# A row softmax on one core: the first tile's load cut into pieces of one, three and twelve rows a partition in place of four and twelve

## The chip, the cores and the metric

The kernel runs on one core of a Trainium2 chip. The metric is the device time of one execution in microseconds (us). Executions of the same kernel agree within about 0.8% here (the kernel with two tiles in one-row pieces varies more); each comparison below was run beside the kernel before on the same chip.

## The reference

```python
x: (16, 1024, 512) float32
x_scaled = x / 0.5
exp_x = np.exp(x_scaled - np.max(x_scaled, axis=-1, keepdims=True))
out = exp_x / np.sum(exp_x, axis=-1, keepdims=True)      # float32
```

There are 16,384 rows of 512 numbers. 33.55 MB come in and 33.55 MB go out, and nothing can be left out: every input byte is read once and every output byte written once.

## The kernel before

The rows are cut into 8 tiles of 128 partitions x 16 rows (4.19 MB each), with six buffers. A tile is worked on in blocks of rows: VectorE takes each row's maximum, ScalarE the exponentials with their sums, VectorE and ScalarE divide the rows of the block before and the one before that, and a tile is stored when its last block is done. The sync queue (SP) issues all loads, ScalarE's queue all stores.

```python
    FIRST = [(0, 4), (4, 16)]                  # pieces in which tile 0 is loaded
    BLOCKS_FIRST = [(0, 4), (4, 4), (8, 8)]    # (first row, rows): blocks of tile 0
    BLOCKS = [(0, 8), (8, 8)]                  # blocks of the other tiles
    data = ctx.enter_context(tc.tile_pool(name="data", bufs=6))
    # ... cut ...
    def load(c):
        xt = tiles[c] = data.tile([P, G, D], fp32, name="xt")
        for lo, hi in FIRST if c == 0 else [(0, G)]:
            nc.sync.dma_start(out=xt[:, lo:hi, :], in_=xr[c][:, lo:hi, :])

    def shift(i):                              # one block
        c, b, B = blocks[i]
        xb = tiles[c][:, b : b + B, :]
        negmax = stats.tile([P, 8], fp32, name="negmax")
        nc.vector.tensor_reduce(negmax[:, 0:B], xb, axis=AX, op=MAX, negate=True)
        # ... cut ...
    def store(i):
        c, b, B = blocks[i]
        if b + B == G:
            nc.scalar.dma_start(out=outr[c], in_=tiles[c])

    for i in range(n + 3):
        if i < n:
            if blocks[i][1] == 0:
                load(blocks[i][0])
            shift(i)
            exponentials(i)
        if 1 <= i <= n:
            scale_vector(i - 1)
        if 2 <= i <= n + 1:
            scale_scalar(i - 2)
        if 3 <= i:
            store(i - 3)
```

Of the kernel before, what the change touches and what calls it, by code (L numbers as in the profile page):

```python
# [1 line left out]

# [4 lines left out]


@with_exitstack
def kernel(  # L10
    ctx: ExitStack,
    tc: tile.TileContext,
    x: bass.AP,
    out: bass.AP,
):
    nc = tc.nc
    fp32 = mybir.dt.float32
    P = nc.NUM_PARTITIONS
    AX = mybir.AxisListType.X
    EXP = mybir.ActivationFunctionType.Exp  # L20
    COPY = mybir.ActivationFunctionType.Copy
    MAX = mybir.AluOpType.max

    D = x.shape[-1]
    xf = x.flatten_outer_dims()
    of = out.flatten_outer_dims()
    N = xf.shape[0]




    G = 16
    C = N // (P * G)
    assert C * P * G == N
    xr = xf.rearrange("(c p g) d -> c p g d", p=P, g=G)
    outr = of.rearrange("(c p g) d -> c p g d", p=P, g=G)

    FIRST = [(0, 4), (4, 16)]
    BLOCKS_FIRST = [(0, 4), (4, 4), (8, 8)]
    BLOCKS = [(0, 8), (8, 8)]  # L40

    data = ctx.enter_context(tc.tile_pool(name="data", bufs=6))
    stats = ctx.enter_context(tc.tile_pool(name="stats", bufs=6))

    ctx.enter_context(tc.manual_schedule())


    warm = stats.tile([P, 1], fp32, name="warm", bufs=1)
    nc.vector.memset(warm, 0.0)  # L49
    nc.scalar.activation(out=warm, in_=warm, func=EXP)  # L50

    tiles = {}
    blocks = [(c, b, B) for c in range(C) for b, B in (BLOCKS if c else BLOCKS_FIRST)]
    state = {}
# [6 lines that stand above are left out]
    def shift(i):  # L61
# [4 lines that stand above are left out]
        bias = stats.tile([P, 8], fp32, name="bias")  # L66
        nc.vector.tensor_scalar_mul(bias[:, 0:B], negmax[:, 0:B], 2.0)  # L67
        state[i] = (xb, bias)

    def exponentials(i):  # L70
        B = blocks[i][2]
        xb, bias = state[i]
        sums = stats.tile([P, 8], fp32, name="sums")
        for g in range(B):
            nc.scalar.activation(  # L75
                out=xb[:, g, :],
                in_=xb[:, g, :],
                func=EXP,
                bias=bias[:, g : g + 1],
                scale=2.0,  # L80
                accum_out=sums[:, g : g + 1],
            )
        state[i] = (xb, sums)

    def scale_vector(i):
        B = blocks[i][2]
        xb, sums = state[i]
        recip = stats.tile([P, 8], fp32, name="recip")
        nc.vector.reciprocal(recip[:, 0:B], sums[:, 0:B])  # L89
        for g in range(B - B // 4):  # L90
            nc.vector.tensor_scalar_mul(xb[:, g, :], xb[:, g, :], recip[:, g : g + 1])  # L91
        state[i] = (xb, recip)

    def scale_scalar(i):
        B = blocks[i][2]
        xb, recip = state[i]
        for g in range(B - B // 4, B):
            nc.scalar.activation(  # L98
                out=xb[:, g, :], in_=xb[:, g, :], func=COPY, scale=recip[:, g : g + 1]
# [7 lines that stand above are left out]
    n = len(blocks)  # L107
# [14 lines that stand above are left out]
# [1 line left out]
_INS = ['x']  # L123
_OUTS = [((16, 1024, 512), 'float32')]


# [23 lines left out]
```

## Time and profile before

The kernel before took 162.37 us, the median of three runs (162.35 to 162.6). The span that the profile covers is about 2 us shorter.

| | value | read from |
|---|---|---|
| span | 160.4 us | page |
| DMA, 2 to 158 us | share 1.00, 430 GB/s | table of windows |
| VectorE (DVE) busy | 114.0 us, 71% | page |
| ScalarE (ACT) busy | 113.1 us, 70% | page |
| first reduction starts | 5.43 us | timeline |
| first store issued | 43.59 us | timeline |

These lines are from the page of the kernel before. The digits are busy tenths in 40 slices of 4.0 us. The lines of q1 (loads) and q10 (stores) give packets, MB, and the time that the packets took as a share of 16 DMA engines' span. The last two lines are the chain of work that ended last, by engine and by line (L65 is the reduction).

```profile
span 160.4 us, 517 instructions
...
DVE  0608999999999999999999949996199946000000
ACT  3072579989999999999999995799709999100000
...
DMA  5999999999999999999999999999999999999993
GB/s 190 464 425 490 392 417 490 403 392 507 409 368 417 386 441 474 392 417 474 417 409 476 417 400 490 417 400 458 441 409 441 458 409 433 458 400 425 474 409 155
DMA packets 2451, 67.13 MB, mean 419 GB/s; under 512 B 272, under 2 KB 272, under 8 KB 272
...
q1 hardware_dynamic: 1296, 33.56, 49.4%
q10 hardware_dynamic: 1152, 33.55, 48.5%
...
DMA 43%; DVE 34%; ACT 7%; issue 1%; SPq 0%
DMA xt<-in_x_dram 24%; DVE negmax L65 23%; DMA out_dram<-xt 19%; DVE xt L91 9%; ACT xt L75 5%; ACT xt L98 2%; DVE bias L67 1%; DVE recip L89 0%; SPq L59 0%
```

DMA reads 9 in 38 of 40 slices, while VectorE and ScalarE have zeros near both ends. (A packet, here one partition's share of a load or store, is counted whole in the slice where it starts, so the GB/s of single slices scatter around the mean.) The two queues sum to 97.9% of 160.4 us: the DMA engines were busy for 157.0 us and idle for 3.4, nearly all of it before the first packet and after the last. The chain names VectorE's reductions with 23% of the span. DMA has more of the chain than any other engine, 43%. A chain shows one path of waits; it doesn't say that the resource it crosses is the one in short supply.

The table of windows has, for one stretch, its length, busy time of VectorE, ScalarE and GpSimd, the clock, the DMA share and GB/s:

```profile
2.00:158.00 156.00, 113.94 (x147) 111.78 (x290) 0.00 (x0) 1.00 1.00 430
```

From the timeline (start us, us, engine, line, operation, idle time before and what ended it):

```profile
0.73 3.43 SPq L59 DMA_DIRECT2D xt<-in_x_dram  x7
...
5.43 2.29 DVE L65 TENSOR_REDUCE negmax<-xt 128x4 f32<-128x2048 f32 x1 [4.57 <-DMA xt<-in_x_dram]
...
43.59 0.37 ACTq L105 DMA_DIRECT2D out_dram<-xt  x1
```

The first seven loads, thus tiles 0 to 5, are issued by 4.16 us, long before the first result. The first store follows at 43.59 us, the last at 137.05 us; no computation comes after it, but packets move until 159.2 us. Until the first store only loads move, and they have some 58 us of transfers to make (25.2 MB at 430 GB/s, an estimate). The list of DMA issues gives count, KB each, and us from issue to landing:

```profile
xt<-in_x_dram SPq DMA_DIRECT2D x1, 3072.0 KB, 11.5
xt<-in_x_dram SPq DMA_DIRECT2D x1, 1024.0 KB, 4.7
```

### The profile page before, as it was taken

How to read it: one execution, taken by the hardware profiler on the slowest of the kernel's cores; microseconds unless marked ns; L12 is line 12 of the kernel's file. 1: busy time of each engine (PE TensorE's matmuls, PEld its weight loads, DVE VectorE, ACT ScalarE, POOL GpSimd, SP SyncE). 2: the span in 40 equal slices, each digit the busy share in tenths (PEclk: the TensorE clock that was granted, in tenths of full speed). 3: DMA queues.
4: the chain of work that ended last, by engine and by line, in shares of the span. 5: the costliest groups of instructions: out<-in, count | busy, mean ns of one | idle time of the engine just before them, and what ended most of it. 6: DMA issues, size and time to landing. Idle time of an engine off the chain costs nothing.

```text
span 160.4 us, 517 instructions
## 1 busy us (share of the span) xinstructions
DVE 114.0 (71%) x148; ACT 113.1 (70%) x290; POOL 0.2 (0%) x4
## 2 busy tenths in 40 slices
DVE  0608999999999999999999949996199946000000
ACT  3072579989999999999999995799709999100000
POOL 0000000000000000000000000000000000000000
DMA  5999999999999999999999999999999999999993
GB/s 190 464 425 490 392 417 490 403 392 507 409 368 417 386 441 474 392 417 474 417 409 476 417 400 490 417 400 458 441 409 441 458 409 433 458 400 425 474 409 155
DMA packets 2451, 67.13 MB, mean 419 GB/s; under 512 B 272, under 2 KB 272, under 8 KB 272
## 3 DMA queue, kind: packets, MB, share of 16 engines
q1 hardware_dynamic: 1296, 33.56, 49.4%
q10 hardware_dynamic: 1152, 33.55, 48.5%
q14 instruction: 3, 0.02, 0.0%
HBM read 33.55 MB, written 33.55 MB: 418 GB/s over the span
## 4 chain that ended last, share of the span: by engine, by line
DMA 43%; DVE 34%; ACT 7%; issue 1%; SPq 0%
DMA xt<-in_x_dram 24%; DVE negmax L65 23%; DMA out_dram<-xt 19%; DVE xt L91 9%; ACT xt L75 5%; ACT xt L98 2%; DVE bias L67 1%; DVE recip L89 0%; SPq L59 0%
## 5 line engine op out<-in xcount | busy, mean ns | idle before, releaser
L75 ACT ACTIVATE xt<-xt,bias 128x512 f32<-128x512 f32 x128 | 90.5, 708 | 23.2 <-DVE bias L67 23.2
L65 DVE TENSOR_REDUCE negmax<-xt 128x8 f32<-128x4096 f32 (+1 forms) x17 | 70.8, 4163 | 16.9 <-DMA xt<-in_x_dram 16.9
L91 DVE TENSOR_SCALAR xt<-xt,recip 128x512 f32<-128x512 f32 x96 | 39.6, 482 | 0.6
L75 ACT ACTIVATION_READ_ACCUMULATOR xt<-xt,bias 128x1 f32 x128 | 23.9, 187 | 0.0
L98 ACT ACTIVATE xt<-xt,recip 128x512 f32<-128x512 f32 x32 | 21.0, 707 | 0.0
L89 DVE RECIPROCAL recip<-sums 128x8 f32<-128x8 f32 (+1 forms) x17 | 3.3, 192 | 3.2 <-ACT xt L75 3.2
L67 DVE TENSOR_SCALAR bias<-negmax 128x8 f32<-128x8 f32 (+1 forms) x17 | 2.9, 171 | 0.6
L50 ACT ACT_TABLE_LOAD x1 | 1.3, 1283 | 0.7 <-PEq L134 0.7
L49 DVE MEMSET warm<- 128x1 f32 x1 | 0.1, 59 | 0.8 <-PEq L134 0.8
L50 ACT ACTIVATE warm<-warm 128x1 f32<-128x1 f32 x1 | 0.2, 203 | 0.0
L134 POOL MEMSET const-bfloat16-1.0<- 128x1 bf16 x1 | 0.1, 102 | 0.0
L134 POOL MEMSET const-uint8-127<- 128x1 uint8 x1 | 0.1, 101 | 0.0
L134 POOL MEMSET const-float32-0.0<- 128x1 f32 x1 | 0.1, 99 | 0.2 <-issue 0.2
L134 POOL MEMSET const-float32-1.0<- 128x1 f32 x1 | 0.1, 98 | 0.0
## 6 DMA issues: line engine op xcount, KB each, us to landing
out_dram<-xt ACTq DMA_DIRECT2D x8, 4096.0 KB, 26.2
xt<-in_x_dram SPq DMA_DIRECT2D x7, 4096.0 KB, 30.3
xt<-in_x_dram SPq DMA_DIRECT2D x1, 3072.0 KB, 11.5
xt<-in_x_dram SPq DMA_DIRECT2D x1, 1024.0 KB, 4.7
```

Of the source, the lines that this page charges most:

```text
L49: nc.vector.memset(warm, 0.0)
L50: nc.scalar.activation(out=warm, in_=warm, func=EXP)
L65: nc.vector.tensor_reduce(negmax[:, 0:B], xb, axis=AX, op=MAX, negate=True)
L67: nc.vector.tensor_scalar_mul(bias[:, 0:B], negmax[:, 0:B], 2.0)
L75: nc.scalar.activation(out=xb[:, g, :], in_=xb[:, g, :], func=EXP, bias=bias[:, g : g + 1], scale=2.0, accum_out=sums[:, g : g + 1],)
L89: nc.vector.reciprocal(recip[:, 0:B], sums[:, 0:B])
L91: nc.vector.tensor_scalar_mul(xb[:, g, :], xb[:, g, :], recip[:, g : g + 1])
L98: nc.scalar.activation(out=xb[:, g, :], in_=xb[:, g, :], func=COPY, scale=recip[:, g : g + 1])
L134: nc = _bacc.Bacc("TRN2", target_bir_lowering=False, num_devices=1)
```

## The change

Its intent is to have the first data land sooner, so that the computation can start sooner. The whole diff:

```diff
-    FIRST = [(0, 4), (4, 16)]
+    FIRST = [(0, 1), (1, 4), (4, 16)]
     BLOCKS_FIRST = [(0, 4), (4, 4), (8, 8)]
```

The blocks stay as they are. The first reduction still covers four rows, and waits for both small pieces.

## The prediction

> **What bounds the kernel now.** The DMA engines. The page's 40 slices show DMA busy 9 (90% or more) in all but the first and the last slice; the table of windows gives a DMA share of 1.00 and 430 GB/s from 2 to 158 us. The program moves 33.55 MB in and 33.55 MB out, and 67.11 MB at 430 GB/s is 156 us of the span of 160.4. The Trainium skill ("Perfetto Trace Analysis", Roofline) gives about 435 GB/s as the most that one core's 16 DMA engines move; the 430 of this trace agrees. VectorE (114.0 us, 71%) and ScalarE (113.1 us, 70%) have slack. The chain of waits passes through 23% VectorE max reductions, but transfers are always queued behind it: six tiles' loads (25 MB, some 58 us) at the start, later stores and loads.
>
> **What the change does.** The compared order of instructions is the same on every compute engine. Only the load queue differs: a load of 128x2048 becomes one of 128x512 and one of 128x1536, so ten loads in place of nine. The block list is unchanged: the first block is still four rows, and the first reduction now waits for two semaphores, those of the one-row piece and of the three-row piece. So no computation can start on the one row early.
>
> **Costs.**
> - DMA time: in the trace an 8 KB packet takes 309 ns and a 24 KB packet 912 ns; the line through them has 7.5 ns fixed per packet (estimate). Each engine handles 8 packets more, 8 x 7.5 ns, and one semaphore write of 9 ns more: about 0.07 us.
> - Issue: one load issue is 0.33 to 0.57 us on the sync queue. The second piece is issued while the first (0.26 MB, about 0.65 us at the busy rate) moves, so I expect no starvation; later loads are issued about 0.4 us later, behind a long backlog.
> - Start-up: the first 1 MB takes about 3.3 us of packets where 8 x 309 ns would be 2.5 us. Smaller packets in this phase may gain or lose a few tenths of a us.
> - Semaphore lanes shift: the sixth tile's load now waits for the one-row piece to land (about 3.5 us). It would have been issued near 4 us anyway, and has some 40 us of transfers ahead of it: nothing.
>
> **On the critical path.** The DMA stream: +0.07 us, with ±0.4 us for start-up. The first reduction starts at 5.43 us before; I expect 5.3 to 5.9 us. VectorE's work up to the first store's issue (43.6 us) may shift by as much, with no effect on the end, because the queue isn't empty.
>
> **Predicted:** 162.45 us, range 161.9 to 163.0. Chance of faster by over 2%: 0.01; within 2%: 0.97; slower by over 2%: 0.02.
>
> **What the profile would show.** 128 packets of 2 KB and 128 of 6 KB in place of 128 of 8 KB; packets up by 144; DMA share 1.00 from 2 to 158 us; the first reduction at 5.3 to 5.9 us after a wait for the load; first store near 43.6 to 44 us; busy times of VectorE and ScalarE unchanged; span 160.2 to 161.
>
> **What would make it wrong.** If the DMA queue runs dry in some stage (then a compute shift of tenths of a us would show at the end, still far under 2%); if small packets at the start stall the engines for longer than the second piece's issue; if the changed semaphore lanes hold back a load or store late in the program; or if another chip runs the same kernel some tenths of a us differently.

## The result, and the profile after

The changed kernel took 162.47 us (median of four runs, 162.33 to 162.5), the kernel before 162.49 us beside it. The ratio is 0.9991, with a 95% interval of 0.9968 to 1.0015: the same. Ratios here are the mean time of one kernel's runs over that of the other's runs of the same rounds, so not quite the ratio of the medians quoted. Executions over 1.5% slower than the fastest of the same kernel are left out of the means.

The same lines of the page, of the changed kernel:

```profile
span 160.7 us, 519 instructions
...
DMA  5999999999999999999999999999999999999993
GB/s 168 467 404 487 424 400 465 434 408 449 441 318 432 443 400 449 457 400 432 457 408 443 449 416 432 457 408 424 465 416 408 465 432 408 449 449 408 449 449 147
DMA packets 2595, 67.13 MB, mean 418 GB/s; under 512 B 288, under 2 KB 288, under 8 KB 544
...
q1 hardware_dynamic: 1440, 33.56, 49.5%
q10 hardware_dynamic: 1152, 33.55, 48.4%
```

There are 144 more packets, all on the load queue: 128 more of data and 16 semaphore writes. The queues sum to 97.9% of 160.7 us, or 157.3 us busy and 3.4 idle, as before. The same window:

```profile
2.00:158.00 156.00, 113.94 (x147) 111.78 (x290) 0.00 (x0) 1.00 1.01 430
```

The timeline and the list of DMA issues of the changed kernel:

```profile
0.73 4.33 SPq L59 DMA_DIRECT2D xt<-in_x_dram  x8
...
6.12 2.29 DVE L65 TENSOR_REDUCE negmax<-xt 128x4 f32<-128x2048 f32 x1 [5.26 <-DMA xt<-in_x_dram]
...
44.24 0.37 ACTq L105 DMA_DIRECT2D out_dram<-xt  x1
```

```profile
xt<-in_x_dram SPq DMA_DIRECT2D x1, 3072.0 KB, 11.7
xt<-in_x_dram SPq DMA_DIRECT2D x1, 768.0 KB, 4.9
xt<-in_x_dram SPq DMA_DIRECT2D x1, 256.0 KB, 2.6
```

The one-row piece landed 2.6 us after its issue, but no computation begins then. The eighth load of the list, tile 5's, is among the eight issued by 5.06 us, so its new wait for the one-row piece did not hold it. One thing is off: the first reduction began at 6.12 us, 0.69 us later than before and later than the 5.3 to 5.9 predicted. The first store came 0.65 us later too. The span grew by only 0.3 us.

### The profile page after: what moved, and what is told of

Its sections match the earlier page's. It is cut to its first block, busy times and chain, and to the rows that moved or that the text cites. A ratio compares the mean times of both kernels' runs of the same rounds, so it can differ in the third digit from the quotient of the medians.

```text
span 160.7 us, 519 instructions
## 1 busy us (share of the span) xinstructions
DVE 114.0 (71%) x148; ACT 113.1 (70%) x290; POOL 0.2 (0%) x4
## 2 busy tenths in 40 slices
DMA packets 2595, 67.13 MB, mean 418 GB/s; under 512 B 288, under 2 KB 288, under 8 KB 544
## 4 chain that ended last, share of the span: by engine, by line
DMA 43%; DVE 34%; ACT 7%; issue 1%; SPq 1%
DMA xt<-in_x_dram 24%; DVE negmax L65 23%; DMA out_dram<-xt 19%; DVE xt L91 9%; ACT xt L75 5%; ACT xt L98 2%; DVE bias L67 1%; SPq L59 1%; DVE recip L89 0%
```

## The experiments

The theory: the 16 DMA engines set the time. They have work queued from the first packet to the last, so moving the computation's start by microseconds, either way, changes nothing, and the change adds only the small cost of more packets. The first rival: the computation's chain sets the time, and the change failed only because no block used the early row. The second rival, about the size: small pieces cost much more, or nothing at all.

### Let a block use the early row

```diff
     FIRST = [(0, 1), (1, 4), (4, 16)]
-    BLOCKS_FIRST = [(0, 4), (4, 4), (8, 8)]
+    BLOCKS_FIRST = [(0, 1), (1, 3), (4, 4), (8, 8)]
```

> The changed kernel, with the first block of four rows cut into one of one row and one of three, so that something uses the one-row piece. Theory (the DMA stream sets the time, and the early row had no user): the first reduction starts near 3.5 us in place of 6.1, and the time stays within 0.3 us of the kernel before, 162.2 to 162.8 us. Rival (the computation's start sets the time, the change only lacked a block to use it): about 2.5 us less, near 160 us.

It took 162.72 us (162.37 to 163.67, six runs) against 162.56, ratio 1.0024 (0.9996 to 1.0053). Its first two reductions and its first store in the timeline:

```profile
3.47 0.69 DVE L65 TENSOR_REDUCE negmax<-xt 128x1 f32<-128x512 f32 x1 [2.61 <-DMA xt<-in_x_dram]
...
5.88 1.75 DVE L65 TENSOR_REDUCE negmax<-xt 128x3 f32<-128x1536 f32 x1 [1.53 <-DMA xt<-in_x_dram]
...
44.09 0.37 ACTq L105 DMA_DIRECT2D out_dram<-xt  x1
```

The computation did start at 3.47 us, 2 us earlier than in the kernel before, and the time did not fall. The rival wanted 160 us. So the missing block explains why nothing started early. But the early start did not travel: the second reduction waited for the three-row piece until 5.88 us, the third for the twelve-row piece until 13.18 us (12.69 before), and the first store came 0.5 us later than in the kernel before. The run shows that an early row alone moves nothing behind the first block; what an earlier first store would be worth, it doesn't test. That the time doesn't hang on the computation's start rests on the delays that follow.

### Start the computation later: first tile in one piece

```diff
-    FIRST = [(0, 4), (4, 16)]
+    FIRST = [(0, 16)]
```

> The kernel before, with the first tile loaded in one piece of sixteen rows, so that the first reduction starts some 7 us later (near 12.5 us). Theory (DMA stream): 162.2 to 162.8 us, first store near 50 us in place of 43.6. Rival (computation's start sets the time): about 169 us.

It took 162.76 us (162.6 to 163.28, four runs), ratio 1.0015 (0.9992 to 1.0038).

```profile
12.98 2.29 DVE L65 TENSOR_REDUCE negmax<-xt 128x4 f32<-128x2048 f32 x1 [12.12 <-DMA xt<-in_x_dram]
...
46.99 0.38 ACTq L105 DMA_DIRECT2D out_dram<-xt  x1
```

The first reduction came 7.55 us later (12.98 against 5.43), the first store only 3.40 us later, not the 6.4 expected: in the kernel before, VectorE waits once more, 4.76 us, for the twelve-row piece, and that wait is gone here. By the end the delay is gone: the last store is issued at 135.74 us, against 137.05, since VectorE waited 2.57 and 4.98 us for the last two tiles before, and 0 and 2.92 us here. The ratio differs from 1 by 0.15%, and its interval holds 1.

### Start it later still, with the same bytes

The first reduction is done four or ten times; the result is the same and so is every load.

```diff
-        nc.vector.tensor_reduce(negmax[:, 0:B], xb, axis=AX, op=MAX, negate=True)
+        for _ in range(4 if i == 0 else 1):       # 10 in the other kernel
+            nc.vector.tensor_reduce(negmax[:, 0:B], xb, axis=AX, op=MAX, negate=True)
```

> The kernel before, with the first reduction done four times, all computation 6.9 us later at its start, no byte changed. In the kernel before, VectorE waits 2.6 and 5.0 us for the last two tiles, and the stores issued at 122.7 us still find some 2 MB queued (bytes issued less bytes moved at 430 GB/s, an estimate), so a delay of about 5 us at the end has room. Theory (DMA stream): the delay is absorbed, 162.2 to 163.2 us. Rival (computation's start sets the time): 169.3 us.

With four it took 162.50 us (162.43 to 162.7, four runs), ratio 0.9997 (0.9973 to 1.0022). Timeline, then page:

```profile
5.39 9.25 DVE L66 TENSOR_REDUCE negmax<-xt 128x4 f32<-128x2048 f32 x4 [4.53 <-DMA xt<-in_x_dram]
...
46.34 0.38 ACTq L106 DMA_DIRECT2D out_dram<-xt  x1
```

```profile
DMA  5999999999999999999999999999999999999994
```

6.9 us of added VectorE work delayed the first store by only 2.75 us, because the 4.76 us wait for the twelve-row piece is gone here too. It cost nothing measurable.

> The kernel before, with the first reduction done ten times (same result), 9 x 2.29 = 20.6 us later for all computation, and no byte changed. Theory (DMA stream, fed by six queued tiles): the loads queued at the start end near 60 us (25.2 MB at 430 GB/s, estimate), the first store is issued near 64 us, so the DMA engines run dry for some 4 us and perhaps once more when the next stores are awaited: 166 to 174 us. Rival (computation's start sets the time): 183 us. If the slack is larger than I think: 162.5 us.

With ten it took 167.39 us (167.28 to 167.57, four runs), ratio 1.0295 (1.0275 to 1.0316). From its page:

```profile
span 165.3 us, 526 instructions
...
DMA  5998999989999989949898999999999899588985
GB/s 194 440 508 381 452 436 404 484 381 492 396 414 468 389 383 428 460 135 412 357 492 381 484 404 422 460 389 500 389 428 452 389 492 396 254 381 381 508 381 254
...
q1 hardware_dynamic: 1296, 33.56, 48.3%
q10 hardware_dynamic: 1152, 33.55, 47.2%
```

Here the slack is used up. The first store went out at 60.32 us in the timeline, 16.7 us later. The 18th slice moves only 135 GB/s, as do later ones 254; the queues sum to 95.5% of 165.3 us, 157.9 busy and 7.4 idle. Busy time grew by 0.9 us, idle time by 4.0. The computation's start does matter once the DMA engines run dry, and only for the part that they run dry. The kernel before stands somewhere between a delay of 3.40 us at the first store that is free (the first tile in one piece) and one of 16.7 us that costs 4.8 us (167.39 less 162.56).

### The cost of small pieces: four, two and one tiles in one-row pieces

```diff
-        for lo, hi in FIRST if c == 0 else [(0, G)]:
+        for lo, hi in [(g, g + 1) for g in range(G)] if c < 4 else [(0, G)]:   # c < 2, c < 1
```

> The kernel before, with the first four tiles each loaded as sixteen one-row pieces (64 loads where there were 5). In the changed kernel's trace a 2 KB packet takes 84 ns (median) and a 32 KB packet 1213 ns. Theory (each packet has a fixed cost, and the DMA stream sets the time): 16 x 84 - 1213 = 131 ns for each of 4 x 8 rows of an engine, 4.2 us, and 60 semaphore writes of 9 ns, 0.5 us: 166 to 168 us. Rival (small packets cost nothing here): 162.5 us. Rival (every further load has a slow start of some 0.5 us that no backlog hides): over 180 us.

It took 171.93 us (171.24 to 172.44, four runs), ratio 1.0571 (1.0543 to 1.0599): 9.4 us more, where 4.7 had been worked out. Its page, a window while the small packets flow, and the same window in the kernel before:

```profile
span 170.3 us, 613 instructions
...
DMA  5999999999999999999999999999999299589892
GB/s 170 324 401 387 387 388 387 386 386 386 451 431 434 442 423 439 431 431 431 433 423 439 423 439 423 439 423 454 416 446 415 123 423 439 246 369 492 369 492 125
...
q1 hardware_dynamic: 9792, 33.56, 50.1%
q10 hardware_dynamic: 1152, 33.55, 45.7%
```

```profile
15.00:35.00 20.00, 19.65 (x24) 15.14 (x42) 0.00 (x0) 1.00 1.05 387
```

```profile
15.00:35.00 20.00, 19.75 (x25) 16.34 (x45) 0.00 (x0) 1.00 0.98 425
```

Small packets run at 387 GB/s with every engine busy. The load queue's share is 50.1% of 170.3 us, 85.3 us, against 49.4% of 160.4, 79.2 us: 6.1 us more instead of 4.7. But a share is a sum of packets' recorded times, and the 1.05 in the first window shows that these overlap while the small packets flow, so part of the 6.1 us is counted twice. Bytes are the safer count. With all data packets of a trace in the order of their ends, this is when so many MB had moved:

```
data moved, MB                             20     35     50    67.1
kernel before, us from the span's start  50.4   84.7  119.5  159.2
one tile in one-row pieces, us behind     1.3    1.7    1.5    1.9
two tiles (slow run), us behind           1.8    2.4    2.4    6.2
four tiles, us behind                     4.0    4.5    4.2    9.2
```

The other two traces of the kernel before lie at most 0.3 us behind at these marks. At 50 MB, long after the last small packet, the kernel with four tiles is 4.2 us behind, near the 4.7 worked out for packets. So the packets' size was about right. What failed is the step that nothing else is lost: the other 5.0 us come after that, where the DMA engines run dry. They show as slices of 123 and 246 GB/s and at the end. (By the shares, idle time is 3.4 us in the kernel before and 7.2 here, 95.8% of 170.3 us being busy; the overlap makes the 7.2 too small.) In this kernel VectorE waits for a tile that comes late, which the kernel before didn't do at that place:

```profile
72.86 4.42 DVE L65 TENSOR_REDUCE negmax<-xt 128x8 f32<-128x4096 f32 x1 [8.53 <-DMA xt<-in_x_dram]
```

The trace shows why that tile, the fifth, is late. From the ninth load on, each load's issue waits for an earlier load to land (56 waits of the sync queue, 19.7 us in all, in the view of waits), so no more than eight small pieces, 2.1 MB, are under way. The fifth tile's load is issued only at 43.5 us, behind the first store at 42.33 us, where the kernel before had issued it by 4.16 us. From 45 to 55 us the store moved 3.5 MB and the loads 0.5 MB; in the kernel before it was 1.4 and 2.3 MB. The pieces thus cost not only time per packet: they also take away the backlog that was to hide later delays.

> The kernel before, with only the first two tiles loaded as sixteen one-row pieces. With four tiles the time rose by 9.3 us, of which 4.7 were predicted; in that trace the stream ran at 387 GB/s while the small packets lasted, and the DMA engines ran dry later, near 132 and 145 us, as the computation got its fifth tile late. Theory (packets' fixed cost, and a second loss once the backlog is used up): here 2 x 8 x 131 ns = 2.1 us, 28 semaphore writes of 9 ns, 0.3 us, and a slow start of about 1 us, with nearly all of the backlog still there: 164.9 to 166 us. Rival (twice the cost per packet, nothing to do with the backlog): half of 9.3, about 167.2 us.

It took 167.57 us, with a wide spread (166.22 to 168.72, four runs; 167.39 is the median of the three fast ones). The profiled run was the slowest, so its trace is only support here. The ratio is 1.0293 (1.0260 to 1.0326), near the rival's 167.2 and outside the theory's range. Yet the rival's mechanism isn't what the trace shows: the load queue's busy time is 49.2% of 166.7 us, 82.0 us, or 2.8 us more than before, close to the 2.4 worked out and not 4.6. Idle time is 6.5 us, 3.1 more. The count of bytes agrees: 2.4 us behind at 50 MB, 3.8 more by the end. So my size for the packets was nearly right, and my claim that the backlog would hide the rest was wrong.

> The kernel before, with only the first tile in sixteen one-row pieces. With two and four tiles, the load queue's busy share of 16 engines times the span was 82.0 and 85.3 us against 79.2, so +2.8 and +6.1 us, the prediction's kind of cost; the rest of the added time, 2.9 us in both, was idle time of the DMA engines late in the program. Theory (packet cost in proportion; idle only where the later loads come late enough to use up the queue): load queue busy +1.4 to 1.8 us, no idle added: 163.7 to 164.5 us. Rival (the idle time comes with the one-row pieces whatever their number): 166 to 167.5 us.

(The "2.9 us in both" of this text is not what the pages give: idle time grew by 3.1 us with two tiles and by 3.8 with four.)

It took 164.10 us (163.55 to 164.32, four runs), ratio 1.0087 (1.0062 to 1.0111), inside the theory's range and well below the rival's.

```profile
span 162.3 us, 540 instructions
...
DMA  4899999999999999999999999999999999999992
GB/s 170 265 398 476 420 420 452 428 406 460 428 422 436 428 436 428 436 436 436 428 444 422 436 436 420 436 436 436 436 420 436 444 412 444 444 420 444 444 412 113
...
q1 hardware_dynamic: 3312, 33.56, 49.4%
q10 hardware_dynamic: 1152, 33.55, 47.9%
```

The sum is right, its parts are not quite: the load queue was busy for 80.2 us, 1.0 more than before (I expected 1.4 to 1.8), and idle time grew by 1.0 us, to 4.4. The idle time sits at the start: the second slice moves 265 GB/s at a busy share of 8, where the kernel before moves 464. All later slices are 9, save the last. In this trace, then, the small pieces at the start left the engines partly without work, while the sync queue waited for pieces to land (1.8 us between 4 and 8 us). With two and four tiles the same slice moves 339 and 324 GB/s at a share of 9, so the size of this loss is not settled. The late idle time of the two other doses is absent.

The 21 us delay shows that late computation by itself empties the queue late in the program. That late loads caused the late computation here is read from one trace with four tiles, and was not isolated by a run; for two tiles, whose trace is of a slow run, it remains open.

### Was the late first reduction real?

> The changed kernel unaltered, to see how far its trace repeats. In the first trace the first reduction started at 6.12 us, 0.69 us later than in the kernel before and later than I had predicted (5.3 to 5.9). If this is a property of the three pieces: 6.0 to 6.3 us again (the one-row experiment gave 5.88 for its second block, the same wait). If it was the chance of one execution: anything between 5.3 and 6.3. Time 162.2 to 162.8 us.

> The kernel before unaltered, for a second trace of it. If the first reduction's start is a property of the program: 5.3 to 5.6 us again. If it is chance: up to 6.2 us. Time 162.1 to 163.1 us.

The changed kernel again: 162.68 us (162.67 to 162.84, five runs), ratio 1.0022 (1.0010 to 1.0035). The kernel before again: 162.28 us, one run, no ratio, and its state is unknown. Their first reductions (the line number is one higher, for a comment line), the changed kernel first:

```profile
5.62 2.29 DVE L66 TENSOR_REDUCE negmax<-xt 128x4 f32<-128x2048 f32 x1 [4.76 <-DMA xt<-in_x_dram]
```

```profile
5.56 2.29 DVE L66 TENSOR_REDUCE negmax<-xt 128x4 f32<-128x2048 f32 x1 [4.71 <-DMA xt<-in_x_dram]
```

6.12 us did not come back; it was 5.62 this time. The same program thus varies by 0.5 us here from one execution to the next, most of the 0.69 us.

> The changed kernel, with the three-row piece issued by ScalarE's queue as its first work, while the sync queue issues the one-row piece; sizes of packets are the same. Theory of the late first reduction (the three-row piece is issued one issue, 0.42 us, later, and only 0.65 us of transfer stand before it): the two issues overlap, the first reduction starts at 5.3 to 5.7 us. Rival (the small packets themselves are slow at the start): near 6.1 us still. The whole time by either: 162.1 to 162.8 us, as the rest of the stream is the same.

```diff
-            nc.sync.dma_start(out=xt[:, lo:hi, :], in_=xr[c][:, lo:hi, :])
+            queue = nc.scalar if (c, lo) == (0, 1) else nc.sync
+            queue.dma_start(out=xt[:, lo:hi, :], in_=xr[c][:, lo:hi, :])
```

The two lines that warm ScalarE up were also moved behind the first load. It took 162.77 us (162.43 to 163.17, six runs), ratio 1.0024 (1.0009 to 1.0040).

```profile
5.57 2.29 DVE L64 TENSOR_REDUCE negmax<-xt 128x4 f32<-128x2048 f32 x1 [4.71 <-DMA xt<-in_x_dram]
```

5.57 us is what the issue theory expected, but as the unaltered changed kernel gave 5.62 in the same set of runs, this tells nothing apart. It is inconclusive, and it brought no gain.

> The kernel before, unaltered but for a comment, timed against itself in five rounds: how small a difference these comparisons can show. Two comparisons of the change gave ratios of 0.9991 (0.9968 to 1.0015) and 1.0022 (1.0010 to 1.0035). If the intervals tell the whole uncertainty: the interval here holds 1.000 and is no wider than 0.3%. If a ratio of 1.002 comes up here too, the second result of the change is no cost of the change.

> The changed kernel a third time, beside the kernel before against itself on the same chip. Theory (fixed cost per packet and a slower start, 0.1 to 0.3 us): ratio 1.0005 to 1.002. Rival (the change is free): as for the kernel before against itself, 0.999 to 1.001. First reduction: 5.5 to 6.2 us, as the three executions so far that wait for the three-row piece from the sync queue gave 6.12, 5.88 and 5.62.

The kernel before against itself: 162.40 us (162.16 to 162.88, six runs), ratio 0.9990 (0.9971 to 1.0009). The changed kernel: 162.63 us (162.31 to 162.9, six runs), ratio 1.0002 (0.9983 to 1.0020). First reductions, the changed kernel first:

```profile
5.73 2.29 DVE L66 TENSOR_REDUCE negmax<-xt 128x4 f32<-128x2048 f32 x1 [4.88 <-DMA xt<-in_x_dram]
```

```profile
5.44 2.29 DVE L66 TENSOR_REDUCE negmax<-xt 128x4 f32<-128x2048 f32 x1 [4.58 <-DMA xt<-in_x_dram]
```

The second ratio's interval leaves out 1; a 1.002 did not come up in the kernel before against itself, so that comparison doesn't explain it away, and its own interval is 0.38% wide, not the 0.3% expected. The third ratio, 1.0002, lies in the rival's range, but its interval holds the theory's too. In three traces each the first reduction started at 5.43, 5.56 and 5.44 us before, and at 6.12, 5.62 and 5.73 after: means of 5.48 and 5.82, so some 0.3 us later, with one value far out. Three more traces have the same wait: the two kernels with delays, loaded as before, gave 5.39 and 5.44 us, and the second block of the early-row kernel 5.88. All four starts behind the three-row piece on the sync queue are later than all five of the kernel before's loads, so a delay of some 0.4 us (the means are 5.45 and 5.84) looks real. The three ratios of the changed kernel are 0.9991, 1.0022 and 1.0002; the kernel before against itself gives 0.9990. The comparison can be off by 0.1% with nothing changed. A cost of 0.1 to 0.3 us is neither shown nor excluded; a gain is not in sight.

## Why the prediction was right

- **The time, 162.45 us predicted and 162.47 measured.** Right, and for the reason given; that the two agree to 0.02 us is luck, as the kernel before alone ranged from 162.35 to 163.01 us beside it. Two kernels delayed the first store by 3.40 and 2.75 us, one began its first block 2 us early without moving the first store forward, and the ratios of all three lie within 0.25% of 1. Only a delay of 16.7 us at the first store showed, and then as idle time of the DMA engines.
- **"No computation can start on the one row early."** Right: the first reduction waited for the three-row piece. But this wasn't the deciding part. With a block that used the row, the time didn't fall either, as the next blocks waited for the next pieces.
- **"Transfers are always queued."** Right for the kernel before and after: busy and idle times of the queues are 157.0 and 3.4 us, 157.3 and 3.4 us. It is a fact about this schedule with a limited margin, as the kernels with gaps show.
- **About 0.07 us of added DMA time.** Not resolvable by the times. The load queue's busy time, share times span, was 79.5, 79.2 and 79.1 us in the three traces of the changed kernel, against 79.2. In the large dose the same kind of term held: 4.2 us behind at 50 MB, where 4.7 had been worked out. What it left out there is the late idle time.
- **First reduction at 5.3 to 5.9 us.** Wrong in the trace that followed (6.12), right in the next two (5.62, 5.73). The spread from one execution to the next, about 0.5 us, was not in the estimate, nor was a start that looks 0.3 to 0.4 us later in the mean. **First store at 43.6 to 44 us** missed likewise (44.24), as it followed the first reduction (0.65 us later after 0.69).
- **Semaphore lanes, packet counts, VectorE's busy time, span.** As predicted: tile 5's load was not held back (the "lanes" are the semaphores that tell of landings; they are used in turn, which made this load wait for the one-row piece to land), 2,451 packets became 2,595, VectorE's busy time stayed 114.0 us, and the span was 160.7 us.

On what was drawn from the Trainium skill: "Perfetto Trace Analysis", section Roofline, puts one core's 16 DMA engines at about 435 GB/s; the traces' 430 GB/s agrees. "DMA: Bandwidth & Descriptors", section Why small descriptors are slow (HBM only), says that each packet carries a small fixed cost on top of its bytes. The traces agree in kind: 387 GB/s with 2 KB packets against 425 with 32 KB packets in the same window.

None of the kernels tried was faster than these two by more than the noise. With the same bytes at the same rate, what is left to gain is the 3.4 us in which the DMA engines are idle, nearly all at the two ends of the program, and cutting the first load didn't change it (3.4 us after).

## What to carry to other kernels

An earlier start of the computation is worth something only if the resource that sets the time was waiting for it; here the DMA engines had work from their first packet to their last, so a somewhat later start did not move the time, and an earlier one could gain 3.4 us at most. To see this, add up the shares of the DMA queues and look for slices below 9, rather than trust the chain of waits, 34% of which ran through VectorE; then delay the suspected chain on purpose and see whether the time follows. When a piece of a load is made smaller, check which instruction waits for it alone, and what waits next: the wait for the next piece can swallow the early start. Many small pieces cost time per packet and can also shrink the backlog of loads, so look for idle time late in the program too. Where shares go above 1.00, count bytes against time instead.

## What the Trainium skill lacked or had wrong

- "DMA: Bandwidth & Descriptors", section Anatomy of one DMA, gives about 2.0 us plus bytes over 436 GB/s for one transfer, measured on the GpSimd path. The skill says elsewhere that every transfer pays the fixed part, but shows no such measurement for the sync queue. Here the one-row piece (256 KB), the first in its queue, took 2.5 to 2.8 us from issue to landing in four traces; the same formula gives 2.6 (an estimate: 2.0 + 0.6).
- The same page, section Rules for kernel authors, advises transfers of 1 MiB and more for bandwidth. It doesn't say what smaller ones cost inside a stream that is already full. Here one piece of 1 MB made into two cost nothing measurable (ratios 0.9991, 1.0022 and 1.0002), one tile in sixteen pieces of 256 KB cost 0.9%, two tiles 2.9% and four tiles 5.7%, the last two with late idle time of the DMA engines in them.
- The same page gives a latency to the first byte, but not how slowly a start with many small pieces runs: 265, 339 and 324 GB/s in the second slice with one, two and four tiles in one-row pieces, against 464.
- Neither that page nor "Perfetto Trace Analysis" says how far the landing of a first load varies from one execution to the next: the same program's first reduction came at 5.62 and 6.12 us.
